# Matmul operand pools first in memory, weight tiles of 1024 values: every operand at one place modulo 256 bytes

## The chip, the cores and the metric

One core of one Trainium2 chip runs the whole program. The metric is the device time of one execution in microseconds (us); three runs of the kernel before are shown below. The trace comes from one profiled execution. Of TensorE's clock this text only uses the granted clock in the profile's rows, at 2.4 GHz where it is full.

## The reference, cut to what matters

A one-layer decoder trunk on 512 tokens of 1024 features, all in float32:

```python
xn = rms_norm(h, g_mix[l])
proj = xn @ w_in[l]                       # 1024 x 2564
...                                       # short conv, dilated attention, forgetting attention, pooling
h = h + jnp.concatenate([ya, yb, yc, yd], axis=-1) @ w_out[l]
h = h + memory_cross_attention(rms_norm(h, g_xa[l]), rms_norm(mem, g_mem[l]), w_xq[l], w_xkv[l], w_xo[l])
h = h + conv_ffn(rms_norm(h, g_ffn[l]), w_up[l], w_ffconv[l], w_down[l])
return rms_norm(h, g_final)
```

Nearly all of the arithmetic is in the dense products with w_in, w_out, w_xq, w_xkv, w_xo, w_up (1024 x 5632) and w_down (2816 x 1024).

## The kernel before

Each float32 operand of a dense product is split in two parts of 12 bits, `hi` and `lo`, and one product becomes three passes of TensorE on float32r tiles: hi by hi, hi by lo, lo by hi (`mm3`, L154 to L156). Weights come in loads. A load is one DMA on SP's queue of 512 KB into a tile `raw`, a cast on ScalarE (ACT) into `whi` (L119), and a subtraction on VectorE (DVE) into `wlo` (L120). The class `Weights` holds these tiles, in rings of 3 (`raw`), 4 (`whi`) and 4 (`wlo`) buffers of 1040 values, 4160 bytes per partition. Successive loads go round the ring.

A matmul instruction has a stationary operand, which PEld loads (128 x 128), and a moving operand, which streams through (up to 512 columns). There are two kinds of dense product:

- feature-major (`pair_gemm`: hc, dq, dk, pl, fq, fk, cb, the projections h1 and h2, xq, and upa and upg): the weights are stationary and the activations move, 512 columns at a time. One load of 512 weight rows and 256 columns feeds 4 chunks x 2 tiles x 3 passes = 24 products, then comes the next load.
- token-major (`token_gemm`: fv, dv, xv, and the down projection dn): the activations are stationary and the weights move, 512 columns in dn, 256 in dv and xv, 260 in fv (256 values and 4 gate columns). xk is feature-major with 256 columns.

In the order of the program: hc has 4 loads, fv 2, dq, dk, dv, pl, fq, fk and cb 2 each, xk and xv 8 each (during the attention over the sequence), h1, xq and h2 8 each, the up projection 44 (for each of 11 steps upa twice, then upg twice), the down projection 22. So 106 loads feed 512-wide products, of which the last 11 of dn feed 18 such and 12 of 256 columns.

**Where the operands lie.** Pools are laid out one after the other in SBUF: `cp` (constants, 11,808 bytes per partition), `wp` (the rings), `ap` (activations in tiles of 4096 bytes), `tp` (temporary tiles of 2048 bytes), then the rest. All sub-tiles used by products start at whole multiples of 512 bytes in their tile (in fv, of 1040). Their places, by the addresses in the built program, modulo 256 bytes:

| tiles | place modulo 256 |
|---|---|
| `ident`, `ones` (in cp) | 128 |
| `raw`, 3 buffers | 160, 224, 32 |
| `whi` and `wlo`, in the order in which loads take their 4 buffers | 96, 32, 224, 160 |
| all activations in `ap` and `tp` (xg, mg, h1g, h2g, y, yx, au, ...) | 96 |

Up to the down projection the loads come in such numbers that, in the up projection, the two loads of upa lie at 96 and 32 and the two of upg at 224 and 160, at each of the 11 steps; dn goes round the four places load by load, starting at 96.

The order of instructions on each engine is set by the Tile scheduler from the program's order, its rings and the `issue_after` marks. Around the first token-major product: `fv` (L503 on) takes its four PSUM banks as two of tag `sc` and two of tag `gm`; the two of `gm` are held by the results `p_hc` until ACT has copied them (`ch`, L408). The row sums of squares of x go over ACT (L347) and DVE to `dg_x` (L287), which TensorE multiplies by ones (`pb_x`, L288) between the products of fv.

```python
raw = wp.tile([P, 1040], F32, tag="raw", name=f"raw_{name}", bufs=3)
hi = wp.tile([P, 1040], F32R, tag="whi", name=f"whi_{name}", bufs=4)
lo = wp.tile([P, 1040], F32R, tag="wlo", name=f"wlo_{name}", bufs=4)
```

Of the kernel before, what the change touches and what calls it, by code (L numbers as in the profile page):

```python
# [18 lines left out]
P = 128  # L19
# [41 lines left out]
def trunk(ctx: ExitStack, tc: tile.TileContext, x, mem, positions, g_mix, w_in, b_forget, w_sconv, w_pool,  # L61
          pool_scale, w_out, g_xa, g_mem, w_xq, w_xkv, w_xo, g_ffn, w_up, w_ffconv, w_down, g_final, cst, out):
    nc = tc.nc

    cp = ctx.enter_context(tc.tile_pool(name="cp", bufs=1))
    wp = ctx.enter_context(tc.tile_pool(name="wp", bufs=3))
    ap = ctx.enter_context(tc.tile_pool(name="ap", bufs=28))
    tp = ctx.enter_context(tc.tile_pool(name="tp", bufs=18))
    sp = ctx.enter_context(tc.tile_pool(name="sp", bufs=8))
    pp = ctx.enter_context(tc.tile_pool(name="pp", bufs=1, space=bass.MemoryType.PSUM))  # L70
# [24 lines left out]

# [1 line left out]
    class Weights:  # L97
        """src [rows in chunks of 128, ..., columns], 1040 values per partition at most, as hi, lo [128, chunks, columns]."""

        def __init__(self, src, name):  # L100
            kk, n = src.shape[0] // P, math.prod(src.shape[1:])
            self.src, self.chunks = src, kk
            raw = wp.tile([P, 1040], F32, tag="raw", name=f"raw_{name}", bufs=3)
            hi = wp.tile([P, 1040], F32R, tag="whi", name=f"whi_{name}", bufs=4)
            lo = wp.tile([P, 1040], F32R, tag="wlo", name=f"wlo_{name}", bufs=4)
            self.raw, self.hi, self.lo = (t[:, : kk * n].rearrange("p (k n) -> p k n", n=n) for t in (raw, hi, lo))

# [20 lines left out]
    class Parts:  # L128
        """Feature-major activations of 12 bits each, [128, tokens] per chunk of 128 features."""

# [13 lines left out]
        def fill(self, c, src, scale=None):  # L144
            """Chunk c from src, times a scale per feature."""
            if scale is None:
                nc.scalar.copy(self.hi[c], src)
                nc.vector.tensor_tensor(self.lo[c], src, f(self.hi[c]), op=ALU.subtract)
            else:
                nc.scalar.activation(self.hi[c], src, AF.Copy, scale=scale)  # L150
                nc.vector.scalar_tensor_tensor(self.lo[c], src, scale, f(self.hi[c]), op0=ALU.mult, op1=ALU.subtract)
# [6 lines left out]
    def pump(gen, n):  # L158
        """The next n pieces of some work; whether there was as much."""
        for _ in range(n):  # L160
            if next(gen, "end") == "end":
                return False
        return True

    def along(main, side):
        """Pieces of side in front of the pieces of main."""
        pump(side, 1)
        for _ in main:
            yield
            pump(side, 1)  # L170
        pump(side, 99)
# [8 lines left out]
    def pair_gemm(src, parts, name, done, width=512, ks=None, tag="gm"):  # L180
        """Two tiles of 128 output features each from src [1024, 256]: psum[n, tokens] = sum over k of W[k, n] a[k, tokens]."""
        if width == 512:
            p_ = [ps(f"p_{name}{j}", tag) for j in range(2)]
        else:
            bank = ps(f"p_{name}", tag)
            p_ = [bank[:, :width], bank[:, width : 2 * width]]
        ks = ks or list(range(KC))
        for half in range(2):
            part = ks[4 * half : 4 * half + 4]
            k0 = min(part)  # L190
            hi, lo = load_split(src[k0 * P : (k0 + 4) * P], f"{name}_{half}")
            for n, k in enumerate(part):
                for j in range(2):
                    cs = slice(j * P, (j + 1) * P)
                    mm3(p_[j], hi[:, k - k0, cs], lo[:, k - k0, cs], parts.hi[k], parts.lo[k], k == ks[0] and (j == 0 or width == 512), k == ks[-1])
                latest_mm[:] = [latest()]
                if n % 2:
                    yield
        if width < 512:
            done(bank)  # L200
            return
        for j in range(2):
            done(j, p_[j])

    def token_gemm(src, parts, blocks, name, done, tags=("gm",) * 4):
        """psum[tokens, n] of each block of tokens, from src [1024, n]; two blocks share a bank where they fit."""
        n = src.shape[1]
        per = 512 // n
        banks = [ps(f"p_{name}{i}", tags[i]) for i in range(blocks // per)]
        p_ = [banks[b // per][:, b % per * n : b % per * n + n] for b in range(blocks)]  # L210
        for half in range(2):
            hi, lo = load_split(src[half * 512 : half * 512 + 512], f"{name}_{half}")
            for k in range(4 * half, 4 * half + 4):
                for b in range(blocks):
                    t = slice(b * P, (b + 1) * P)
                    kk = k % 4
                    nc.tensor.matmul(p_[b], parts.hi[k][:, t], hi[:, kk, :], start=k == 0 and b % per == 0, stop=False, skip_group_check=per > 1)  # L217
                    nc.tensor.matmul(p_[b], parts.lo[k][:, t], hi[:, kk, :], start=False, stop=False, skip_group_check=per > 1)
                    nc.tensor.matmul(p_[b], parts.hi[k][:, t], lo[:, kk, :], start=False, stop=k == KC - 1, skip_group_check=per > 1)
                if k % 2:  # L220
                    yield
        for b in range(blocks):
            done(b, p_[b])

# [1 line left out]
    rows0 = cp.tile([8, P], F32, name="rows0")  # L226
# [39 lines left out]
    def rsqrt_small(ss, name, n):  # L266
        """1 / sqrt(ss / D + eps) for a [128, n] of sums of squares."""
        v = small(f"v_{name}", n)
# [13 lines left out]
    def row_broadcast(r, name, tag):  # L282
        """[128 tokens, blocks] to [128, tokens], the same on each partition."""
        pb = ps(f"pb_{name}", tag)
# [7 lines left out]

# [1 line left out]
    def rope_tables():  # L294
# [24 lines left out]

# [1 line left out]
    pv = ps("pv0", "po")  # L321

    def keep_warm(n):
        """The tensor engine's clock falls when it idles and rises after some work: products of ones."""
        for i in range(n):
# [105 lines left out]

# [1 line left out]
    pv = ps("pv", "tr")  # L433
# [6 lines left out]

# [1 line left out]
    y = Parts("y", KC)  # L442
# [52 lines left out]

# [1 line left out]
    fox = {}  # L497
# [62 lines left out]

# [1 line left out]
    pool_sums = []  # L562
# [40 lines left out]

# [1 line left out]
    mem_ = {}  # L605
# [50 lines left out]

# [1 line left out]
    def attention(runs, rest):  # L658
        """runs: mixers with the first of their chunks of y and their biases; rest: what TensorE does between."""
        steps = [(name, pair, i, first, bias_of) for name, first, bias_of in runs for pair in range(2) for i in range(NB)]  # L660
        st, es, po = {}, {}, {}

        def stack(name, pair):
            """Each head's queries as [hi; lo] and its keys' hi and lo twice, over all 128 rows."""
            for hh in range(2):
# [96 lines left out]

# [1 line left out]
    class Project:  # L764
# [42 lines left out]

# [1 line left out]
    (kT_hi, kT_lo), vm_hi, vm_lo = mem_["kT"], mem_["vh"], mem_["vl"]  # L809
# [89 lines left out]

# [1 line left out]
    SPLIT_EARLY = 10  # L901
# [47 lines left out]
    def h2_tokens(n):  # L949
        """Half of a block of the residual, token-major."""  # L950
        if n < 2 * NB:
# [27 lines left out]

# [1 line left out]
    gfin = flat(act4("gfin"))  # L981
# [3 lines left out]
    def finish(b, half, c0, c1):  # L985
        """The residual and the sum of squares of some columns of a half of a block."""
        o = h2t[b][:, 512 * half + c0 : 512 * half + c1]
# [6 lines left out]
    def scale_out(b, ssq):  # L994
        """1 / rms by a step of Newton's, times -2; gfin has the -1 / 2."""
        s = small(f"s_o{b}", 1)
# [65 lines left out]
```

## Time and profile before

| | |
|---|---|
| time, median of 3 runs | 754.33 us (754.23 to 754.98) |
| span of the profiled execution | 752.2 us |
| time around the span (median less span) | 2.1 us |
| PE busy / PEld busy | 742.5 us (99%) / 620.8 us (83%) |
| DVE / ACT / POOL busy | 428.6 / 339.4 / 127.8 us |
| granted clock, mean | 0.997 |
| read from HBM, written | 73.46 MB, 4.27 MB |

The profiled execution has no time of its own beside its span in the record; the sums below are made against the span, and the 2.1 us are carried along. The profile models a matmul's end, so its "mean ns of one" overlaps with the next matmul; what a product costs on TensorE is the step from its start to the next one's start, which the timeline gives. Of a run of products without a break the mean step is the difference of two starts, divided by the number of products between them.

### The profile page before, as it was taken

The page shows a single profiled execution, that of the slowest core. Times are in us where ns is not written, and L with a number is a line of the kernel's source. Part 1 is how long each engine was busy: PE and PEld are TensorE (multiplying, and loading weights), DVE is VectorE, ACT ScalarE, POOL GpSimd, SP SyncE. Part 2 cuts the span into 40 slices and gives each one's busy share as a digit, 9 for nine tenths or more (in the row PEclk, how much of TensorE's full clock was granted, in tenths as well). Part 3 has the DMA queues.
Part 4 walks back from the last instruction along what each step waited for, and adds up shares of the span by engine and source line. Part 5 has one row for each costly group of instructions (what it writes and reads, how often), then busy time and mean ns, then how long its engine had stood idle before and what let it go on. Part 6 is the DMA issues. An engine that isn't in the chain of part 4 may idle for free.

```text
span 752.2 us, 9886 instructions
## 1 busy us (share of the span) xinstructions
PE 742.5 (99%) x3809; PEld 620.8 (83%) x3809; DVE 428.6 (57%) x723; ACT 339.4 (45%) x581; POOL 127.8 (17%) x140
## 2 busy tenths in 40 slices
PE   8999999999999999999999999999999999999996
PEld 7898877899988888888888888888888888888885
DVE  4868576768635436546546656666565567323214
ACT  4773654678634434444335334343333335213214
POOL 5233040033303300001211110111100114003000
PEclk9999999999999999999999999999999999999998
DMA  9743512233434422102322232232332322423202
GB/s 297 228 131 107 169 58 83 85 114 113 147 120 126 139 86 85 56 29 65 104 84 85 85 112 85 92 99 90 103 94 90 107 84 85 140 86 111 85 0 112
DMA packets 67711, 78.37 MB, mean 104 GB/s; under 512 B 3038, under 2 KB 58886, under 8 KB 67664
## 3 DMA queue, kind: packets, MB, share of 16 engines
q1 hardware_dynamic: 65040, 71.33, 30.5%
q0 software_dynamic: 2032, 5.36, 2.2%
q10 hardware_dynamic: 592, 1.05, 0.4%
q8 instruction: 30, 0.49, 0.3%
q14 instruction: 17, 0.14, 0.1%
HBM read 73.46 MB, written 4.27 MB: 103 GB/s over the span
## 4 chain that ended last, share of the span: by engine, by line
PE 98%; DMA 1%; ACT 0%; DVE 0%; issue 0%; SPq 0%; ACTq 0%
PE p_upg L154 5%; PE p_upg L156 5%; PE p_upg L155 5%; PE p_upa L154 5%; PE p_upa L155 5%; PE p_upa L156 5%; PE p_dn L154 5%; PE p_dn L156 5%; PE p_dn L155 5%; PE p_h L155 4%; PE p_h L154 4%; PE p_h L156 4%; PE p_xq L154 2%; PE p_xq L155 2%; PE p_xq L156 2%; PE p_xv L217 1%
## 5 line engine op out<-in xcount | busy, mean ns | idle before, releaser
L154 PE MATMUL p_upg<-h2g_hi,whi_upg 128*128 128x512 f32 x176 | 70.0, 398 | 0.0
L156 PE MATMUL p_upg<-h2g_hi,wlo_upg 128*128 128x512 f32 x176 | 69.5, 395 | 0.0
L155 PE MATMUL p_upg<-h2g_lo,whi_upg 128*128 128x512 f32 x176 | 69.5, 395 | 0.0
L154 PE MATMUL p_upa<-h2g_hi,whi_upa 128*128 128x512 f32 x176 | 69.2, 393 | 0.0
L155 PE MATMUL p_upa<-h2g_lo,whi_upa 128*128 128x512 f32 x176 | 68.9, 391 | 0.0
L156 PE MATMUL p_upa<-h2g_hi,wlo_upa 128*128 128x512 f32 x176 | 68.6, 390 | 0.0
L154 PE MATMUL p_dn<-whi_dn,au_hi 128*128 128x512 f32 (+1 forms) x176 | 66.7, 379 | 0.0
L156 PE MATMUL p_dn<-whi_dn,au_lo 128*128 128x512 f32 (+1 forms) x176 | 66.7, 379 | 0.0
L155 PE MATMUL p_dn<-wlo_dn,au_hi 128*128 128x512 f32 (+1 forms) x176 | 66.5, 378 | 0.0
L120 DVE TENSOR_TENSOR wlo_dn<-raw_dn,whi_dn 128x1024 fp32r<-128x1024 f32 x22 | 27.6, 1256 | 59.1 <-ACT whi_dn L119 59.0
L119 ACT CAST whi_upg<-raw_upg 128x1024 fp32r<-128x1024 f32 x22 | 23.1, 1049 | 79.3 <-PE p_upg L155 66.0
L119 ACT CAST whi_dn<-raw_dn 128x1024 fp32r<-128x1024 f32 x22 | 23.1, 1049 | 72.4 <-PE p_dn L156 30.2
L788 POOL TENSOR_TENSOR acc_h<-acc_h,sq_h 128x512 f32<-128x512 f32 x14 | 21.8, 1559 | 150.2 <-ACT sq_h L787 150.0
L943 POOL TENSOR_TENSOR au<-uo_a,sg 128x512 f32<-128x512 f32 x12 | 23.2, 1938 | 116.1 <-ACT sg L933 116.1
L120 DVE TENSOR_TENSOR wlo_upg<-raw_upg,whi_upg 128x1024 fp32r<-128x1024 f32 x22 | 27.0, 1225 | 23.2 <-ACT whi_upg L119 23.2
L156 PEld LDWEIGHTS p_upg<-h2g_hi,wlo_upg 128*128 128x128 f32 x176 | 33.1, 188 | 7.9
L154 PEld LDWEIGHTS p_upg<-h2g_hi,whi_upg 128*128 128x128 f32 x176 | 33.1, 188 | 7.7
L155 PEld LDWEIGHTS p_upg<-h2g_lo,whi_upg 128*128 128x128 f32 x176 | 33.1, 188 | 7.6
L156 PEld LDWEIGHTS p_upa<-h2g_hi,wlo_upa 128*128 128x128 f32 x176 | 33.0, 188 | 7.3
L154 PEld LDWEIGHTS p_upa<-h2g_hi,whi_upa 128*128 128x128 f32 x176 | 33.1, 188 | 7.1
L155 PEld LDWEIGHTS p_upa<-h2g_lo,whi_upa 128*128 128x128 f32 x176 | 33.1, 188 | 6.8
L156 PEld LDWEIGHTS p_dn<-whi_dn,au_lo 128*128 128x128 f32 x176 | 33.0, 188 | 6.7
(407 smaller groups left out, 1944.2 us busy)
## 6 DMA issues: line engine op xcount, KB each, us to landing
raw_upa<-in_w_up_dram SPq DMA_DIRECT2D x22, 512.0 KB, 3.6
raw_upg<-in_w_up_dram SPq DMA_DIRECT2D x22, 512.0 KB, 3.5
raw_dn<-in_w_down_dram SPq DMA_DIRECT2D x22, 512.0 KB, 3.8
raw_xk<-in_w_xkv_dram SPq DMA_DIRECT2D x8, 512.0 KB, 3.4
raw_xv<-in_w_xkv_dram SPq DMA_DIRECT2D x8, 512.0 KB, 3.6
raw_h<-in_w_out_dram SPq DMA_DIRECT2D x8, 512.0 KB, 3.5
raw_xq<-in_w_xq_dram SPq DMA_DIRECT2D x8, 512.0 KB, 3.5
raw_h<-in_w_xo_dram SPq DMA_DIRECT2D x8, 512.0 KB, 3.4
```

What stands on the lines that cost most here:

```text
L119: nc.scalar.copy(self.hi[:, ks], self.raw[:, ks])
L120: nc.vector.tensor_tensor(self.lo[:, ks], self.raw[:, ks], f(self.hi[:, ks]), op=ALU.subtract)
L154: nc.tensor.matmul(psum, ah, bh, start=first, stop=False, skip_group_check=True)
L155: nc.tensor.matmul(psum, ah, bl, start=False, stop=False, skip_group_check=True)
L156: nc.tensor.matmul(psum, al, bh, start=False, stop=last, skip_group_check=True)
L217: nc.tensor.matmul(p_[b], parts.hi[k][:, t], hi[:, kk, :], start=k == 0 and b % per == 0, stop=False, skip_group_check=per > 1)
L788: nc.gpsimd.tensor_tensor(acc, acc, sq, op=ALU.add)
L943: nc.gpsimd.tensor_tensor(au[i][:, j, :], ff.pop(("a", c)), sg, op=ALU.mult)
```

## The change

Pool `cp` is opened after `wp`, `ap` and `tp`. The tiles of a load have 1024 values instead of 1040, so a buffer of a ring is 4096 bytes, and a row of n weights takes a pitch of n rounded up to 64 values. With 260 columns (fv) the pitch is 320, so that 3 chunks of 128 rows fit in a tile, not 4: fv is loaded in 3 parts (3, 3 and 2 chunks) instead of 2. All other loads keep their shapes. Comments and docstrings are dropped as well.

```diff
-    cp = ctx.enter_context(tc.tile_pool(name="cp", bufs=1))
     wp = ctx.enter_context(tc.tile_pool(name="wp", bufs=3))
     ap = ctx.enter_context(tc.tile_pool(name="ap", bufs=28))
     tp = ctx.enter_context(tc.tile_pool(name="tp", bufs=18))
+    cp = ctx.enter_context(tc.tile_pool(name="cp", bufs=1))
...
-            raw = wp.tile([P, 1040], F32, tag="raw", name=f"raw_{name}", bufs=3)
-            hi = wp.tile([P, 1040], F32R, tag="whi", name=f"whi_{name}", bufs=4)
-            lo = wp.tile([P, 1040], F32R, tag="wlo", name=f"wlo_{name}", bufs=4)
-            self.raw, self.hi, self.lo = (t[:, : kk * n].rearrange("p (k n) -> p k n", n=n) for t in (raw, hi, lo))
+            raw = wp.tile([P, 1024], F32, tag="raw", name=f"raw_{name}", bufs=3)
+            hi = wp.tile([P, 1024], F32R, tag="whi", name=f"whi_{name}", bufs=4)
+            lo = wp.tile([P, 1024], F32R, tag="wlo", name=f"wlo_{name}", bufs=4)
+            pitch = -(-n // 64) * 64
+            self.raw, self.hi, self.lo = (t[:, : kk * pitch].rearrange("p (k n) -> p k n", n=pitch)[:, :, :n] for t in (raw, hi, lo))
...
-        for half in range(2):
-            hi, lo = load_split(src[half * 512 : half * 512 + 512], f"{name}_{half}")
-            for k in range(4 * half, 4 * half + 4):
+        step = 1024 // (-(-n // 64) * 64)
+        for k0 in range(0, KC, step):
+            k1 = min(k0 + step, KC)
+            hi, lo = load_split(src[k0 * P : k1 * P], f"{name}_{k0}")
+            for k in range(k0, k1):
...
-                    kk = k % 4
+                    kk = k - k0
```

By the addresses of the built program, `raw`, all four buffers of `whi` and of `wlo`, all tiles of `ap` and `tp`, and `ident` and `ones` then lie at 128 modulo 256. Line numbers after the change are 2 to 4 higher.

The change moves instructions in one place, around fv. ACT casts weights in the order of arrival; here are its rows from the first cast of fv to the first of eight squares of x, before (`ch` is the copy out of `p_hc`, `junk_x` a square of x).

```order
L119 CAST whi_fv_521<-raw_fv_520 128x1040
L119 CAST whi_fv_575<-raw_fv_574 128x1040
L408 COPY ch_411<-p_hc_144 128x512
L119 CAST whi_dq_657<-raw_dq_656 128x1024
L408 COPY ch_415<-p_hc_145 128x512
L347 ACTIVATE junk_x_419,ssx<-x_cols_88 128x256
```

And the same place of ACT's queue in the changed kernel:

```order
L121 CAST whi_fv_521<-raw_fv_520 128x3x260
L121 CAST whi_fv_563<-raw_fv_562 128x3x260
L121 CAST whi_fv_605<-raw_fv_604 128x2x260
L412 COPY ch_411<-p_hc_144 128x512
L412 COPY ch_415<-p_hc_145 128x512
L351 ACTIVATE junk_x_419,ssx<-x_cols_88 128x256
```

The third cast of fv now stands in front of both copies out of `p_hc`, and the first cast of dq has gone behind the squares of x. On SP's queue, before:

```order
L111 DMA raw_fv_520<-in_w_in_dram 128x4x260
L111 DMA raw_fv_574<-in_w_in_dram 128x4x260
L421 DMA m_tok_449<-in_mem_dram 128x1024
L421 DMA m_tok_450<-in_mem_dram 128x1024
L111 DMA raw_dq_656<-in_w_in_dram 128x4x256
```

and in the changed kernel:

```order
L113 DMA raw_fv_520<-in_w_in_dram 128x3x260
L113 DMA raw_fv_562<-in_w_in_dram 128x3x260
L425 DMA m_tok_449<-in_mem_dram 128x1024
L425 DMA m_tok_450<-in_mem_dram 128x1024
L113 DMA raw_fv_604<-in_w_in_dram 128x2x260
L113 DMA raw_dq_662<-in_w_in_dram 128x4x256
```

The third part of fv takes the place of dq's first load in the ring of `raw`, and every later load moves back by one buffer. On TensorE's queue `pb_x` moves 9 products of fv forward; the rest stands as it stood.

## Rows read from the trace of the kernel before

**Rows 1.** The page: span, busy time, chain that ended last

```profile
span 752.2 us, 9886 instructions
PE 742.5 (99%) x3809; PEld 620.8 (83%) x3809; DVE 428.6 (57%) x723; ACT 339.4 (45%) x581; POOL 127.8 (17%) x140
...
PE 98%; DMA 1%; ACT 0%; DVE 0%; issue 0%; SPq 0%; ACTq 0%
```

**Rows 2.** What TensorE waited for: longest and shortest of three (us, times, longest)

```profile
PE pt_x L354 <- DMA x_cols<-in_x_dram: 1.5, 1, 1.5
...
PE p_fk L154 <- DVE fqT L484: 0.3, 1, 0.3
```

**Rows 3.** The page's groups: one of the nine largest

```profile
L154 PE MATMUL p_upg<-h2g_hi,whi_upg 128*128 128x512 f32 x176 | 70.0, 398 | 0.0
```

**Rows 4.** PE's timeline, one step of the up projection: start, modelled us, what

```profile
556.85 0.39 PE L154 MATMUL p_upa<-h2g_hi,whi_upa 128*128 128x512 f32 x1
...
558.90 0.39 PE L154 MATMUL p_upa<-h2g_hi,whi_upa 128*128 128x512 f32 x1
...
562.30 0.39 PE L154 MATMUL p_upa<-h2g_hi,whi_upa 128*128 128x512 f32 x1
...
567.80 0.40 PE L154 MATMUL p_upg<-h2g_hi,whi_upg 128*128 128x512 f32 x1
...
573.39 0.39 PE L154 MATMUL p_upg<-h2g_hi,whi_upg 128*128 128x512 f32 x1
...
578.99 0.39 PE L154 MATMUL p_upa<-h2g_hi,whi_upa 128*128 128x512 f32 x1
```

**Rows 5.** PE's timeline, four loads of the down projection: first product of each

```profile
645.38 0.40 PE L154 MATMUL p_dn<-whi_dn,au_hi 128*128 128x512 f32 x1
...
650.87 0.39 PE L154 MATMUL p_dn<-whi_dn,au_hi 128*128 128x512 f32 x1
...
656.47 0.39 PE L154 MATMUL p_dn<-whi_dn,au_hi 128*128 128x512 f32 x1
...
662.04 0.39 PE L154 MATMUL p_dn<-whi_dn,au_hi 128*128 128x512 f32 x1
...
667.54 0.40 PE L154 MATMUL p_dn<-whi_dn,au_hi 128*128 128x512 f32 x1
```

**Rows 6.** PE's timeline, 256 columns: xv's first load, then its second

```profile
178.24 0.28 PE L217 MATMUL p_xv<-whi_xv,mg_hi 128*128 128x256 f32 x1
...
179.55 0.28 PE L219 MATMUL p_xv<-wlo_xv,mg_hi 128*128 128x256 f32 x1
...
181.04 0.28 PE L219 MATMUL p_xv<-wlo_xv,mg_hi 128*128 128x256 f32 x1
...
181.72 0.28 PE L219 MATMUL p_xv<-wlo_xv,mg_hi 128*128 128x256 f32 x1
```

**Rows 7.** PE's timeline: eight transposes and the product after them

```profile
188.46 1.03 PE L702 MATMUL ptp_f<-ident,e_f 128*128 128x128 f32 x8
189.25 0.36 PE L217 MATMUL p_xv<-whi_xv,mg_hi 128*128 128x256 f32 x1
```

**Rows 8.** Timelines of SP, ACT, DVE and PE around fv

```profile
29.55 4.47 SPq L111 DMA_DIRECT2D raw_dq<-in_w_in_dram  x2
...
30.98 2.01 ACT L119 CAST whi_fv<-raw_fv 128x1040 fp32r<-128x1040 f32 x2
...
34.53 0.58 ACT L408 COPY ch<-p_hc 128x512 f32<-128x512 f32 x1
...
41.74 0.88 DVE L287 TENSOR_SCALAR dg_x<-ident,r_x 128x128 f32<-128x128 f32 x4
...
36.03 0.28 PE L217 MATMUL p_fv<-whi_fv,xg_hi 128*128 128x260 f32 x1
...
43.91 1.05 PE L288 MATMUL pb_x<-dg_x,ones 128*128 128x128 f32 x8
```

**Rows 9.** The tile raw_dq: its transfers' time from issue to landing

```profile
DMA to landing us min/median/max: 4.0/4.2/4.5
```

## The prediction

> **What bounds the kernel now.** The page comes first: TensorE is busy for 742.5 of 752.2 us, and the chain that ended last is 98% TensorE [rows 1]. Then the waits: the longest that TensorE has on anything is 1.5 us, at the start, and after the first weights there is one of 0.3 us [rows 2]. So no engine, queue or transfer is to be relieved; the time is the sum of TensorE's steps, and only a shorter step can shorten it. The page's groups don't show steps, since their 398 ns are modelled and overlap [rows 3]. The timeline does: the reader should take the start of the first product of each load and subtract.
>
> One step of the up projection [rows 4] has four loads of 24 products of 512 columns, with the moving activations always at 96 modulo 256 and the stationary weights at 96, 32, 224 and 160. They take 562.30 - 556.85 = 5.45, then 5.50, 5.59 and 5.60 us: 227, 229, 233 and 233 ns per product. Nothing else differs between these loads: same shapes, no wait, no other tile's work in between. In the down projection [rows 5] the roles are swapped, activations stationary at 96 and weights moving at 96, 32, 224, 160; the loads take 5.49, 5.60, 5.57 and 5.50 us. The place 32 is fast as a stationary one (5.50) and slow as a moving one (5.60), and with 160 it is the other way round (5.60 and 5.50). What fits all eight is the distance, place of the stationary less place of the moving operand: 0 gives 5.45 and 5.49, 192 gives 5.50 and 5.50, 128 gives 5.59 and 5.57, 64 gives 5.60 and 5.60. A weight buffer's number, a load's turn or the stage don't fit them. So the step depends on where the two operands lie against each other, and distance 0, which the change gives to all, is the best of the four seen.
>
> **The change part by part.**
>
> *512-wide products.* Four loads, one at each place, take 22.14 us in the up projection and 22.16 in the down one; at 5.45 each they take 21.80. The saving is 0.34 us per set of four. There are 106 loads, the last 11 of them with 18 of 24 such products, so 103.25 load equivalents or 25.8 sets: 8.8 us if all settle as these do. Not all do. The load at 645.38, at distance 0, took 5.49 and not 5.45: a stretch at distance 0 starts unsettled, and inside the load at 556.85 the last 15 products step at (562.30 - 558.90) / 15 = 227 ns against 228 for the first nine [rows 4]. The 63.25 equivalents of up and down, mostly unbroken, give 15.8 x 0.34 = 5.4 us. The other 40 loads (hc, dq to cb, h1, xq, h2) have transposes, attention and other tiles' products between theirs, so they start anew often; of their 10 x 0.34 = 3.4 us I take 70%, 2.4. Sum: 7.8 us. The ends: 5.4 + 1.2 = 6.6 (a third of it in the broken stages), and 8.8 + 0.8 = 9.6 (no load starts unsettled any more, which saves up to 0.03 us on the 27 loads that already are at 0).
>
> *256-wide products.* Here distance 0 isn't the best. xv's first load (moving weights at 96) steps at (179.55 - 178.24) / 11 = 119 ns, its second (at 32, distance 64) at (181.72 - 181.04) / 6 = 113 ns [rows 6]. By the code, loads at distance 64 feed 132 such products (xv 48, xk 48, the end of dn 36). 132 x 6 ns = 0.8 us **lost**; ends 0 and 1.3 (a further 180 at distance 192, at most 3 ns each). fv's 260 columns, at mixed places now, step like the others (36.03 to 43.91 for 66 products [rows 8], 119 ns): 0.
>
> *Transposes.* 192 of them (L354, L617, L702, L852, L957) go from a distance of -32 to 0, which no row shows. Eight take 0.79 us to the next product's start, 99 ns each [rows 7]. Above, I bound their cost by the 6 ns between best and worst place of a 256-wide product: 192 x 6 ns = 1.2 us; below by the same as a gain. I take 0, the middle, since no row tells the sign.
>
> *fv in three parts.* One more DMA, cast and subtraction, and ACT's third cast of fv stands ahead of the two copies that free the PSUM banks of fv. The third transfer is issued where dq's first one was, at 29.55, and dq's took 4.0 to 4.5 us [rows 8, 9]; with half its bytes I estimate a landing at 33 to 34. ACT has finished the first two casts by 30.98 + 2.01 less a quarter, some 32.5. So the cast ends between 33.6 and 34.6, and the two copies, 0.58 each, by 34.8 to 35.8. The bank of the second copy is wanted at 36.03 [rows 8], so nothing waits, with 0.2 to 1.2 us in hand. If the cover goes, a landing 1 us later costs 0.8 us. Behind the copies on ACT are the squares of x, and behind these DVE's `dg_x`, done at 42.62 and wanted at 43.91, now some 1.1 us earlier (9 products of 119 ns): 0.2 us in hand. But dq's first cast, 1.05 us, no longer stands between the copies, and the third cast is half of that. I take 0 for all of it; ends 0 and 1.5. The later loads lose one buffer's turn and keep several us of lead.
>
> *The constants' move and the new `raw` places* change no instruction; the work is on DMA queues, ACT and DVE, which TensorE doesn't wait for [rows 2]. 0.
>
> **Sum:** 7.8 - 0.8 = 7.0 us less: span 745.2, and with the 2.1 us around it 747.3, against the median of 754.33 (-0.9%).
>
> The Trainium skill speaks against this change: "TensorE: Matmul & The Clock Gate", Step-by-step, says that TensorE reads its moving and its stationary operand through two independent ports, and Part 1 of the page gives a step of 512 columns as 215.7 ns at full clock. By it an operand's place would be no term at all and the sum would be 0. The trace disagrees on both: 227 to 233 ns, in the order of the distance.
>
> **The rivals.**
>
> *Nothing changes.* The pace belongs to something that goes with the loads' turn, not to the place. For it: upa and upg always have the same two places, so in the up projection turn and place can't be told apart. Against it: dn, where the turn and the pace part company. Time 754.3; chance 0.08.
>
> *Slower.* The pace hangs on the absolute place as well. All operands that now pair have 32 modulo 64; none has the 128 that all get, so only shifts by 64 are covered by the argument above. If 128 on both sides settles like the worst pair, 5.60 per load, then against the present mean of (5.45 + 5.50 + 5.59 + 5.60) / 4 = 5.535 it costs 0.065 x 103 = 6.7 us: 761.0. It decides from 5.535 us per load, 231 ns a product, upward. Against it: the pairs (160, 96) and (96, 32) have the same distance at shifted places and the same 5.60. Chance 0.08.
>
> *Part of the gain is given back*: broken stages gain little, transposes and 256-wide products lose at their ends, fv's third part delays `p_fv` or `pb_x`. 6.6 - 1.3 - 1.2 - 1.5 = 2.6 us: 751.7. Chance 0.1.
>
> *Much faster.* Starts on a multiple of 128 also remove what is left above the column time, 512 / 2.4 GHz = 213 ns: 106 loads with some 2,480 products x 13 ns = 32 us beyond the forecast, 715. Nothing in the rows points to it; chance 0.03.
>
> **How the numbers follow.** My forecast case, the distance decides, has 0.71: 747.3, with its own range of 744.0 (9.6 saved and a transpose or two gained) to 751. The range to 752.0 takes in the third rival and leaves out 0.08 + 0.08 + 0.03. A measurement of this kernel tells some 0.2%, 1.5 us, from no change. Faster: 0.71 + 0.1 + 0.03, less 0.02 for partial gains under 1.5 us = 0.82; same 0.08 + 0.02 = 0.1; slower 0.08.
>
> **What would show it.** Right: in the timeline every load of 24 products in up and down takes 5.44 to 5.46 us, upg's as upa's, and PE's busy time falls by some 7 us with its 3809 instructions unchanged; xv's second load steps at 119 ns; PE's waits stay under 3 us in sum; eight transposes still take 0.79. Wrong: loads that still alternate between 5.45 and 5.60 (nothing changed), or all at 5.55 and more (the absolute place counts); a new wait of PE on ACT's `ch` or DVE's `dg_x` in the first 50 us (fv's third part).

## The result and the profile after

The changed kernel takes 745.93 us (median of 4 runs, 745.46 to 746.99), the kernel before 754.28 us on the same chip (4 runs, 753.82 to 754.98). The ratio is 0.9895, with a 95% interval of 0.9878 to 0.9912: 1.1% faster, by some 8 us where 7.0 were forecast, and inside the range of 744.0 to 752.0.

The page of the changed kernel (span and engines, the chain that ended last, one of its groups) answers to [rows 1, 3]:

```profile
span 745.3 us, 9893 instructions
...
PE 735.8 (99%) x3809; PEld 622.0 (83%) x3809; DVE 430.1 (58%) x724; ACT 339.7 (46%) x582; POOL 131.7 (18%) x140
...
PE 98%; DMA 1%; ACT 0%; DVE 0%; issue 0%; SPq 0%; ACTq 0%
...
L156 PE MATMUL p_upg<-h2g_hi,whi_upg 128*128 128x512 f32 x176 | 69.0, 392 | 0.0
```

TensorE has the same 3809 matmuls and is still busy for 99% of the span; its busy time fell by 6.7 us and the span by 6.9. So the gain is in the steps themselves, and nothing else became the bound. The waits of TensorE say the same (us, times, longest); against [rows 2] there is no wait that the change made, and the 0.3 us on `p_fk` is gone:

```profile
PE pt_x L358 <- DMA x_cols<-in_x_dram: 1.7, 1, 1.7
PE pv L330 <- POOL ones L235: 1.2, 1, 1.2
```

The steps are in TensorE's timeline of the changed kernel (start, modelled us, what). First the start of each load in one step of the up projection, as in [rows 4], then the same of four loads of the down projection, as in [rows 5]:

```profile
552.62 0.39 PE L156 MATMUL p_upa<-h2g_hi,whi_upa 128*128 128x512 f32 x1
...
558.06 0.39 PE L156 MATMUL p_upa<-h2g_hi,whi_upa 128*128 128x512 f32 x1
...
563.50 0.39 PE L156 MATMUL p_upg<-h2g_hi,whi_upg 128*128 128x512 f32 x1
...
568.94 0.39 PE L156 MATMUL p_upg<-h2g_hi,whi_upg 128*128 128x512 f32 x1
...
574.38 0.39 PE L156 MATMUL p_upa<-h2g_hi,whi_upa 128*128 128x512 f32 x1
...
639.66 0.39 PE L156 MATMUL p_dn<-whi_dn,au_hi 128*128 128x512 f32 x1
...
645.10 0.39 PE L156 MATMUL p_dn<-whi_dn,au_hi 128*128 128x512 f32 x1
...
650.54 0.39 PE L156 MATMUL p_dn<-whi_dn,au_hi 128*128 128x512 f32 x1
...
655.98 0.39 PE L156 MATMUL p_dn<-whi_dn,au_hi 128*128 128x512 f32 x1
...
661.42 0.39 PE L156 MATMUL p_dn<-whi_dn,au_hi 128*128 128x512 f32 x1
```

The pattern of 5.45, 5.50, 5.59, 5.60 is gone from both: every load shown takes 5.44 us, 226.7 ns a product. (Early loads of the up projection that begin behind transposes take 5.56 to 5.59 us; from its 17th load on all take 5.44.)

Where the time went is seen by setting the two timelines side by side at the first product of a stage (after less before, us). Below zero the changed kernel is ahead; the third column is what the stretch from the line above added:

| first product of | difference | this stretch |
|---|---|---|
| hc's second load | +0.96 | +0.96, the start |
| dv | +0.45 | -0.51, hc, fv, dq and dk |
| the up projection | -1.55 | -2.00, dv to h2, with xk and xv |
| the down projection | -5.37 | -3.82 |
| its last three loads, which run as one | -6.74 | -1.37 |
| end of the span | -6.93 | -0.19 |

### The profile page after: what moved, and what is told of

It reads as the page before. It is cut to its first block, busy times and chain, and to the rows that moved or that the text cites. A ratio compares the mean times of both kernels' runs of the same rounds, so it can differ in the third digit from the quotient of the medians.

```text
span 745.3 us, 9893 instructions
## 1 busy us (share of the span) xinstructions
PE 735.8 (99%) x3809; PEld 622.0 (83%) x3809; DVE 430.1 (58%) x724; ACT 339.7 (46%) x582; POOL 131.7 (18%) x140
## 4 chain that ended last, share of the span: by engine, by line
PE 98%; DMA 1%; ACT 0%; DVE 0%; issue 0%; SPq 0%; ACTq 0%
PE p_upg L156 5%; PE p_upg L158 5%; PE p_upa L158 5%; PE p_upa L156 5%; PE p_upg L157 5%; PE p_upa L157 5%; PE p_dn L157 5%; PE p_dn L158 5%; PE p_dn L156 5%; PE p_h L157 4%; PE p_h L158 4%; PE p_h L156 4%; PE p_xq L156 2%; PE p_xq L157 2%; PE p_xq L158 2%; PE p_xv L221 1%
## 5 line engine op out<-in xcount | busy, mean ns | idle before, releaser
L156 PEld LDWEIGHTS p_dn<-whi_dn,au_hi 128*128 128x128 f32 x176 | 33.1, 188 | 6.2
```

The source lines that it names most:

```text
L156: nc.tensor.matmul(psum, ah, bh, start=first, stop=False, skip_group_check=True)
```

## The experiments

Five accounts of the gain were on the table. *Distance*: a product's step depends on the place of its stationary operand less that of its moving operand, modulo 256, and 0 is good. *Absolute place*: 128 itself is what is good. *Pools or fv*: the order of the pools, or fv's third part, takes a share of the result. *Constancy*: any one distance for all loads would do, and it is the going round that costs. *History*: a load's pace depends on how it was entered as well as on its distance.

### e1: tile length alone

Before, with tiles of 1088 values: 4352 bytes, a multiple of 256, so all operands lie at 160; `cp` stays first, fv in two parts.

```diff
-            raw = wp.tile([P, 1040], F32, tag="raw", name=f"raw_{name}", bufs=3)
-            hi = wp.tile([P, 1040], F32R, tag="whi", name=f"whi_{name}", bufs=4)
-            lo = wp.tile([P, 1040], F32R, tag="wlo", name=f"wlo_{name}", bufs=4)
+            raw = wp.tile([P, 1088], F32, tag="raw", name=f"raw_{name}", bufs=3)
+            hi = wp.tile([P, 1088], F32R, tag="whi", name=f"whi_{name}", bufs=4)
+            lo = wp.tile([P, 1088], F32R, tag="wlo", name=f"wlo_{name}", bufs=4)
```

> The kernel before with one edit: weight tiles of 1088 values (4352 bytes, 17 x 256) instead of 1040. Constants stay first in memory, fv stays in two parts; all matmul operands then lie at 160 modulo 256, the constants at 128. Theory (the distance between stationary and moving operand sets the step, 0 is best of the four): all of the gain, 745 to 747 us, loads of 24 products at 5.44 us in up and down. Rival A (the absolute place counts, a multiple of 128 is needed): no more than a third of the gain, 751 us or more. Rival B (the pools' order in memory counts): no gain, 754.

Measured: 746.76 us (744.7 to 748.0) against 753.6 of the kernel before, ratio 0.9909 (0.9885 to 0.9933). Four loads of the up projection, from TensorE's timeline of this kernel:

```profile
550.25 0.39 PE L154 MATMUL p_upa<-h2g_hi,whi_upa 128*128 128x512 f32 x1
...
572.01 0.39 PE L154 MATMUL p_upa<-h2g_hi,whi_upa 128*128 128x512 f32 x1
```

(572.01 - 550.25) / 4 = 5.44 us: three changed numbers give nearly the whole effect. Behind the start (from hc's second load to the end of the span) the kernel before takes 736.2 us, e1 729.0 and the changed kernel 728.3; where the last 0.7 comes from is told under e2.

### e2: the change without the move of the pool

```diff
+    cp = ctx.enter_context(tc.tile_pool(name="cp", bufs=1))
     wp = ctx.enter_context(tc.tile_pool(name="wp", bufs=3))
     ap = ctx.enter_context(tc.tile_pool(name="ap", bufs=28))
     tp = ctx.enter_context(tc.tile_pool(name="tp", bufs=18))
-    cp = ctx.enter_context(tc.tile_pool(name="cp", bufs=1))
```

> The change with its first part undone: constants first in memory again, weight tiles of 1024 values kept. All matmul operands lie at 160 modulo 256, the constants at 128; fv in three parts. Theory (distance): as the changed kernel, 745 to 747 us, and the difference to the kernel with 1088-value tiles is the price of fv's third part, 0 to 0.5 us. Rivals A (absolute place) and B (pool order): 751 to 754 us.

Measured: 744.41 us (743.78 to 745.25), ratio 0.9881 (0.9862 to 0.9899). Two neighbouring loads of the up projection, with all operands at 160:

```profile
555.03 0.39 PE L156 MATMUL p_upa<-h2g_hi,whi_upa 128*128 128x512 f32 x1
...
560.47 0.39 PE L156 MATMUL p_upa<-h2g_hi,whi_upa 128*128 128x512 f32 x1
```

That is 5.44 us again. So the absolute place is not what counts: 128 and 160 give the same step. And e1 and e2, which differ in fv's parts, have spans of 743.0 and 742.9 us: fv's third part costs nothing. It even saves a little. Behind the start e2 takes 728.3 us against 729.0, and 0.5 of that is a wait of TensorE which e1 has, with fv in two parts, and which no kernel with three parts has; in the kernel before it was 0.3 us [rows 2]:

```profile
PE p_fk L154 <- DVE fqT L484: 0.5, 1, 0.5
```

### e3: the move of the pool alone

Before, with the line of `cp` put behind `tp`; tiles of 1040 as they were.

```diff
-    cp = ctx.enter_context(tc.tile_pool(name="cp", bufs=1))
     wp = ctx.enter_context(tc.tile_pool(name="wp", bufs=3))
     ap = ctx.enter_context(tc.tile_pool(name="ap", bufs=28))
     tp = ctx.enter_context(tc.tile_pool(name="tp", bufs=18))
+    cp = ctx.enter_context(tc.tile_pool(name="cp", bufs=1))
```

> The kernel before with the other part of the change alone: constants behind the operands' pools, weight tiles still 1040 values, so that the four weight buffers lie at distances 0, 64, 128 and 192 of the activations. Theory (distance): no gain, 753.5 to 755 us, loads that still take 5.45, 5.50, 5.59 and 5.60 us. Rival B (pool order counts): 746 to 750 us.

Measured: 754.1 us (10 runs), ratio 1.0003 (0.9986 to 1.0019). All places are shifted, the distances are not, and the four loads of the up projection keep their old pattern:

```profile
555.09 0.39 PE L154 MATMUL p_upa<-h2g_hi,whi_upa 128*128 128x512 f32 x1
...
560.54 0.39 PE L154 MATMUL p_upa<-h2g_hi,whi_upa 128*128 128x512 f32 x1
...
566.04 0.40 PE L154 MATMUL p_upg<-h2g_hi,whi_upg 128*128 128x512 f32 x1
...
571.63 0.39 PE L154 MATMUL p_upg<-h2g_hi,whi_upg 128*128 128x512 f32 x1
...
577.23 0.39 PE L154 MATMUL p_upa<-h2g_hi,whi_upa 128*128 128x512 f32 x1
```

5.45, 5.50, 5.59 and 5.60, as in [rows 4]. The pool's move has no part in the gain.

### e4 and e6: every distance, up and down

The change, with `hi` and `lo` of each load of the up projection shifted inside longer tiles: 0 to 248 bytes by 8, load after load (e4), the same backwards (e6), then four odd ones. Ten shifts were given to the first loads of the down projection too, and in e6 eight to xk and xv.

```diff
+    def shift_of(name):
+        if name.startswith("up"):
+            i, half = name[3:].split("_")
+            n = 4 * int(i) + 2 * (name[2] == "g") + int(half)
+            return 0 if n < 8 else 2 * (n - 8) if n < 40 else (1, 17, 33, 49)[n - 40]
+        if name.startswith("dn0"):
+            return (0, 4, 8, 12, 16, 24, 32, 40, 48, 56, 60)[int(name[3:])]
+        return 0
...
-            hi = wp.tile([P, 1024], F32R, tag="whi", name=f"whi_{name}", bufs=4)
-            lo = wp.tile([P, 1024], F32R, tag="wlo", name=f"wlo_{name}", bufs=4)
+            hi = wp.tile([P, 1088], F32R, tag="whi", name=f"whi_{name}", bufs=4)
+            lo = wp.tile([P, 1088], F32R, tag="wlo", name=f"wlo_{name}", bufs=4)
...
+            o = shift_of(name)
+            self.raw, self.hi, self.lo = (t[:, s : s + kk * pitch].rearrange("p (k n) -> p k n", n=pitch)[:, :, :n] for t, s in ((raw, 0), (hi, o), (lo, o)))
```

> The changed kernel with the parts of the weights shifted inside tiles of 1088 values, by another amount for each load of the up projection: 32 loads at 0, 8, 16, ... 248 bytes, four at 4, 68, 132 and 196, eight at 0; and for the first half of the down projection at 0, 16, 32, 48, 64, 96, 128, 160, 192, 224, 240 bytes. What is read is each load's settled step. Theory (distance): in up 227 ns at 0, 233 at 64, 232.5 at 128, 229 at 192; in down, with the roles swapped, 229 at 64 and 233 at 192; between these no value is known, I expect values between 226 and 236. Rival C (what counts is that the distance stays the same from load to load, not its value): 227 ns at every shift after the first products of a load. Rival A (absolute place): the steps follow the weights' own place with the same values in up and down.

In e6 `shift_of` reads so:

```diff
-            return 0 if n < 8 else 2 * (n - 8) if n < 40 else (1, 17, 33, 49)[n - 40]
+            return 0 if n < 8 else 2 * (39 - n) if n < 40 else (33, 31, 29, 35)[n - 40]
...
-            return (0, 4, 8, 12, 16, 24, 32, 40, 48, 56, 60)[int(name[3:])]
+            return (0, 60, 56, 48, 40, 32, 24, 16, 12, 8, 4)[int(name[3:])]
+        if name.startswith(("xk", "xv")):
+            g, half = name[2:].split("_")
+            return 8 * (2 * int(g) + (half != "0"))
```

> The scan once more with the same 32 shifts of the up projection in the opposite order (248 down to 0 bytes) and the last four at 132, 124, 116 and 140; the down projection's shifts in the opposite order; and the 16 loads of the 256-wide products xk and xv at 0, 32, 64, ... 224 bytes, twice. Theory in its strict form (the distance alone fixes the settled step): each distance repeats its step of the first scan within 0.5 ns, in particular 226.7 at 0, 120 and 132 bytes and 234.4 at 96. Rival D (the settled step also hangs on the state that the load begins in): several distances settle at another value than in the first scan. Distance 0 has always come to 226.7, so both expect that. For the 256-wide products I expect 119 to 120 ns at 0 and 113 to 118 at some others.

Measured, one run each: 752.29 and 752.89 us. What counts is the settled step, (start of a load's 24th product less start of its 11th) / 13 in the timeline. In the up projection, ns, forward and backward where they differ by 0.6 or more:

| distance | ns | distance | ns | distance | ns | distance | ns |
|---|---|---|---|---|---|---|---|
| 0 | 226.7 | 64 | 233.2 | 128 | 233 | 192 | 229 |
| 8 | 231 | 72 | 233.3 | 136 | 233.3 | 200 | 230.8 |
| 16 | 233.3 | 80 | 232 | 144 | 233.3 | 208 | 232.2 |
| 24 | 231.2 | 88 | 233.4 | 152 | 231.4 | 216 | **231.8, 226.7** |
| 32 | 233.3 | 96 | 234.5 | 160 | 233.4 | 224 | 233.2 |
| 40 | **233.2, 226.7** | 104 | 233.3 | 168 | 233.5 | 232 | 231.2 |
| 48 | 233.4 | 112 | 233.4 | 176 | 230 | 240 | **228.1, 226.6** |
| 56 | 233.3 | 120 | 226.7 | 184 | 232 | 248 | 233.3 |

Three things follow. Distance 0 is at the floor, and the four distances that the kernel before happened to use (0, 192, 128, 64) come out as they stood there. 0 is not alone: 120 gives 226.7 in both scans, and 132, one of the odd ones, 226.6 and 226.7. No load of any run settled below 226.6. And the distance alone doesn't fix the step everywhere: 40, 216 and 240 settled at one pace going up and at another going down. TensorE's timeline of e4 at distance 40, over 23 products, and of e6 at 40, over 24:

```profile
448.73 0.40 PE L167 MATMUL p_upa<-h2g_lo,whi_upa 128*128 128x512 f32 x1
...
454.10 0.40 PE L166 MATMUL p_upg<-h2g_hi,whi_upg 128*128 128x512 f32 x1
```

```profile
567.01 0.39 PE L169 MATMUL p_upg<-h2g_hi,whi_upg 128*128 128x512 f32 x1
...
572.46 0.39 PE L169 MATMUL p_upg<-h2g_hi,whi_upg 128*128 128x512 f32 x1
```

5.37 / 23 = 233.5 ns against 5.45 / 24 = 227. Same shapes, same distance, no wait in either; e4's load began right behind four transposes, e6's without a break. A break isn't needed for that, though: at 216 both loads followed another load without one, and they settled at 231.8 and 226.7 ns; the load before had distance 208 in e4 and 224 in e6. Whether the load before decides isn't shown. So the history account holds for a few distances; that it decides at all of them falls, since the other 29 came out within 0.6 ns of each other in both directions. In the down projection, where the weights move, the picture is the same: 0 at the floor, 229 at 192, 233 to 234 at most others. The absolute place falls here as well: weights shifted by 64 bytes step at 233.2 ns where they are stationary (distance 64) and at 229 where they move (distance 192), and at a shift of 192 it is the other way round, 229 and 233.4. The 256-wide products of e6 stepped (mean of a load's steps under 130 ns) between 116.5 ns (xv at distance 64) and 120.1 (xv at 160), with 118.5 at 0 and 117.0 at 224 in both xk and xv; the 113 ns that were expected at some place did not come.

### e5: steady distances, but not 0

The change, with all weights of up, dn, h1, h2 and xq shifted by 96 bytes: distance 96, and 160 in dn, where the weights move.

```diff
+    def shift_of(name):
+        return 24 if name.startswith(("up", "dn", "h1", "h2", "xq")) else 0
```

> The changed kernel with the weights' parts shifted by 96 bytes, the same for every load of h1, xq, h2, the up and the down projection (90 of the 106 loads of 512-wide products), in tiles of 1088 values. The distance is now constant, 96 in the feature-major loads and 160 in the down projection, where the scan's settled steps were 234.4 and 233.7 ns against 226.7 at 0. Theory (distance): slower than the kernel before, by the settled steps 1632 products x 6.8 ns + 462 x 6.4 ns = 14 us over the changed kernel, 758 to 760 us. Rival C (a constant distance is what helps): as the changed kernel, 744 to 747 us.

Measured: 759.07 us (758.35 to 761.21) against 753.56, ratio 1.0085 (1.0057 to 1.0113): slower than the kernel before, where the change is faster. From TensorE's timeline, 24 products of the up projection and four loads of the down projection:

```profile
504.11 0.40 PE L160 MATMUL p_upg<-h2g_hi,whi_upg 128*128 128x512 f32 x1
...
509.73 0.40 PE L160 MATMUL p_upg<-h2g_hi,whi_upg 128*128 128x512 f32 x1
...
639.00 0.39 PE L160 MATMUL p_dn<-whi_dn,au_hi 128*128 128x512 f32 x1
...
661.40 0.39 PE L160 MATMUL p_dn<-whi_dn,au_hi 128*128 128x512 f32 x1
```

5.62 us per load in up and 22.40 / 4 = 5.60 in dn. All operands of a kind lie at one place, as in the change, and the time moves the other way: constancy is worth nothing by itself.

### e7 and e8: another distance for the 256-wide products, and the change again

The change, with xk's weights shifted by 224 bytes and those of xv and dv by 32, which is distance 224 for all three (their roles differ).

```diff
+    def shift_of(name):
+        return 56 if name.startswith("xk") else 8 if name.startswith(("xv", "dv")) else 0
```

> The changed kernel with the weights of the 256-wide products alone moved off distance 0: xk by 224 bytes, xv and dv by 32, so that their distance is 224, in tiles of 1088 values. In the backward scan such products stepped at 117.0 ns at 224 against 118.5 to 120 at 0. Theory: 480 products x 2 ns = 1 us off the changed kernel, all of it in the stretches of dv, xk and xv, and 512-wide products as before at 226.7. That is less than one measurement of this kernel tells apart; what decides is the steps in the trace. Rival (the interruptions by attention's products set these steps): no change in the steps, 0 us.

e8 is the change itself, beside it.

> The changed kernel itself once more, beside the kernel above on the same chip, with more rounds. Theory: 744 to 747 us, a ratio of 0.987 to 0.991 to the kernel before; in its profile, up's loads at 5.44 us each. If fv's third part cost anything, PE would wait for ACT's ch or DVE's dg_x in the first 50 us; expected 0.

Measured: e7 744.05 us (743.17 to 745.08), ratio 0.9881 (0.9865 to 0.9897); e8 744.74 us (744.29 to 746.45), ratio 0.989 (0.9875 to 0.9904). Twelve products of xv's first load in e7, and then in the changed kernel's first profile:

```profile
174.79 0.28 PE L225 MATMUL p_xv<-whi_xv,mg_hi 128*128 128x256 f32 x1
...
176.08 0.28 PE L227 MATMUL p_xv<-wlo_xv,mg_hi 128*128 128x256 f32 x1
```

```profile
178.37 0.28 PE L221 MATMUL p_xv<-whi_xv,mg_hi 128*128 128x256 f32 x1
...
179.68 0.28 PE L223 MATMUL p_xv<-wlo_xv,mg_hi 128*128 128x256 f32 x1
```

1.29 / 11 = 117 ns against 1.31 / 11 = 119. Over the 480 products of dv, xk and xv, the mean of the steps under 130 ns (some 440 in each kernel, the unbroken ones) is 117.0 ns in e7 against 119.4 in e8, and the stretch from dv to h1 is 0.88 us shorter in e7. That part is shown by the traces; the run times of the two overlap and can't tell it. In e8 TensorE waits for `x_cols` and `ones` alone, as in the first profile, and not for `ch` or `dg_x`.

## Why the prediction was right

**The bound and the mechanism.** Right: the time is TensorE's steps, and a step hangs on the distance of its operands. The absolute place as what decides fell with e2 and the scans, constancy with e5, and "nothing changes" with the changed profile and with e3 beside e1. Of a gain given back only the 256-wide share, which was foreseen, was seen. The prediction called 0 the best of four; in the scans it is one of three (with 120 and 132) of the 39 tried that came to the floor each time, and no better one was found. The Trainium skill's "TensorE: Matmul & The Clock Gate", Step-by-step, says that the two operands are read through two independent ports. The prediction took from it that the place would be no term; the runs don't bear that out: 226.7 to 234.5 ns for the same product at full clock, and 14 us of the kernel's time between the medians of e8 and e5.

**Up and down projection.** 5.4 us forecast; from the first product of up to the end of the span the lead grew by 6.93 - 1.55 = 5.4 us, dn's 256-wide loss of 0.2 included.

**The other 512-wide stages.** The prediction took 70% of a ceiling of 3.4 us, 2.4, since such loads start anew often. From hc's second load to the up projection the lead grew by 0.96 + 1.55 = 2.5 us. The steps of the 512-wide products in that stretch sum to 2.6 us less, 77% of the ceiling. The 256-wide ones lost 0.6, and the rest comes from breaks, mostly the wait before `p_fk` that is gone. But the share is not even: the 24 loads of h1, h2 and xq gained 2.0 us, all of their 24 x 0.085 (0.34 / 4 us a load), while the 15 loads of hc to cb behind the first gained 0.6 of some 1.3, about half. A start at distance 0 takes some ten uneven steps to settle (235, 233, 236, 224, 231, 236, 228, 233, 230, then 227 ns in one load of the up projection behind transposes), which fits that share; no run shows it apart.

**256-wide products.** 0.8 us lost was forecast; the steps of all 256-wide products, attention's among them, sum to 91.53 us before and 92.34 after. xv's second load now steps at 119 ns where it took 113 [rows 6]:

```profile
180.94 0.28 PE L221 MATMUL p_xv<-whi_xv,mg_hi 128*128 128x256 f32 x1
...
181.89 0.28 PE L223 MATMUL p_xv<-wlo_xv,mg_hi 128*128 128x256 f32 x1
```

**Transposes.** 0 was taken between ±1.2 us. Eight of them, to the next product, take 0.80 us where they took 0.79 [rows 7]:

```profile
188.70 1.04 PE L706 MATMUL ptp_f<-ident,e_f 128*128 128x128 f32 x8
189.50 0.36 PE L221 MATMUL p_xv<-whi_xv,mg_hi 128*128 128x256 f32 x1
```

**fv in three parts.** 0 was taken, with 0.2 to 1.2 us in hand. The timelines of SP, ACT, DVE and PE around it, as in [rows 8]:

```profile
30.46 0.38 SPq L113 DMA_DIRECT2D raw_fv<-in_w_in_dram  x1
...
31.89 2.12 ACT L121 CAST whi_fv<-raw_fv 128x780 fp32r<-128x780 f32 x3
...
33.92 1.07 ACT L412 COPY ch<-p_hc 128x512 f32<-128x512 f32 x2
...
42.30 0.88 DVE L291 TENSOR_SCALAR dg_x<-ident,r_x 128x128 f32<-128x128 f32 x4
...
36.89 0.28 PE L221 MATMUL p_fv<-whi_fv,xg_hi 128*128 128x260 f32 x1
...
43.65 1.05 PE L292 MATMUL pb_x<-dg_x,ones 128*128 128x128 f32 x8
```

The copies out of `p_hc` end at 33.92 + 1.07 = 34.99; the product that wants the second bank starts at 36.89, so 1.9 us are in hand. `dg_x` is done at 43.18 and wanted at 43.65: 0.5 us. The cover held at both places. The term itself was not 0 but a gain of 0.3 us: with three parts TensorE no longer waits for DVE's `fqT` before `p_fk` (e1, e2). The prediction had only asked what the third part could cost.

**Forecast and result.** The sum of 7.0 stands against 6.9 in the two profiled spans, but that agreement is partly luck: behind the start the changed kernel gained 7.9 us, and the start, which no term covered, took 1.0 back (below). The 0.9 over the forecast is 0.2 in up and down, 0.2 in the other 512-wide stages and some 0.5 in breaks between products, the wait before `p_fk` above all. In time the forecast was 747.3 and the median 745.93. Every run whose span is on record takes about 1.7 us more than its span; the 2.1 us that the forecast carried along set a median against the span of another run.

## What to carry to other kernels

Where TensorE is the bound and its unbroken products of one shape step unevenly, take the steps per load from the timeline and set them against the operands' addresses; here places modulo 256 made anything from 226.7 to 234.5 ns out of the same float32r product. Tiles whose length is a multiple of 256 bytes, so that both operands lie at the same place, were nearly all that the gain needed (e1), and a common place alone does not help if the distance is a bad one (e5). Price such a change per load from loads that already have the new distance; loads cut up by other products kept about half of it, unbroken ones all.

## What the runs showed that was not expected

**The start differs by up to 2.2 us from run to run, and the granted clock sets it.** hc's first twelve products, to the next transpose, take 5.10 us in the changed kernel's first profile, 4.33 in the kernel before, and 2.86 in e2, the same instructions each time. Their first and the transposes behind them, in that order of kernels:

```profile
7.86 2.05 PE L156 MATMUL p_hc<-xg_hi,whi_hc 128*128 128x512 f32 x4
...
12.96 0.60 PE L358 MATMUL pt_x<-ident,x_cols 128*128 128x128 f32 x4
```

```profile
7.66 2.06 PE L154 MATMUL p_hc<-xg_hi,whi_hc 128*128 128x512 f32 x4
...
11.99 0.60 PE L354 MATMUL pt_x<-ident,x_cols 128*128 128x128 f32 x4
```

```profile
7.72 1.17 PE L156 MATMUL p_hc<-xg_hi,whi_hc 128*128 128x512 f32 x4
...
10.58 0.60 PE L358 MATMUL pt_x<-ident,x_cols 128*128 128x128 f32 x4
```

The slow ones step at 427 ns, which is 512 columns at 1.2 GHz. The windows of the changed kernel's first profile show a granted clock of 1.00 in that stretch (third value from the end), but there they can't be trusted: that trace's first clock record begins at 12.72 us, and a stretch without a record is shown as 1.00. The second profile of the same program, e8, has records there: full from 5.47 us, half from 8.89, full again from 12.30. Its seven slow products lie between. First the window of the changed kernel, then two of e8:

```profile
10.00:12.00 2.00, 2.00 (x6) 1.52 (x6) 1.41 (x3) 0.62 (x1) 0.97 (x2) 1.00 1.10 360
```

```profile
8.00:10.00 2.00, 2.00 (x9) 1.58 (x8) 1.08 (x3) 1.21 (x2) 1.53 (x4) 0.72 1.10 373
10.00:12.00 2.00, 2.00 (x6) 1.54 (x5) 1.23 (x3) 0.62 (x1) 1.11 (x3) 0.50 1.11 349
```

The other runs agree. Where the first record of full clock begins at 10.85 us (before), 11.25 (e4), 12.72 (the changed kernel) and 13.48 (e6), the slow steps end there; in the five runs where full clock is on record from 4.4 to 5.6 us on and stays (e1, e2, e3, e5, e7), no product of hc is slow. So how many products are slow differs from run to run of the same program (ten in one profile of the change, seven in the other), at 0.2 us each, with the moment from which the clock is granted in full. Before e8's fell, TensorE had waited 2.2 us for `x_cols`. Why the moment differs isn't shown. The profiled run of the change, 746.99 us, was the slowest of its four. Spans should be compared behind the start.

**Open.** Why the distance matters, why 120 and 132 are as good as 0, and why a few distances have two paces, no run tells. Nor does any show what holds the last 13 ns between the floor of 226.6 and the column time of 213 (512 / 2.4 GHz); the rival in which they go fell. A best distance for the 256-wide end of dn was not tried.
